# A hybrid encoder step on one core: the second block of the first unit's up weights is loaded early, into two staging tiles

## The chip, the cores and the metric

The kernel runs on 1 core of a Trainium2 chip. The metric is the device time of one execution in microseconds (us); lower is better. The core has TensorE (PE in the profile; PEld is its weight loads), VectorE (DVE), ScalarE (ACT), GpSimd (POOL) and SyncE (SP). SP starts most of the loads and POOL most of the stores. Each engine works through its own list of instructions in order and waits where an instruction needs something that another engine has not yet finished.

## The reference

One inference step of a 2-layer streaming encoder with width 1024, on 1024 prompt frames and 8 x 16 sample frames, 1152 tokens together. Each layer is a mixer (attention, and in layer 0 a convolution too), an output projection with a residual, and then an MLP with a residual:

```python
def rmsnorm(x, g):
    xf = x.astype(jnp.float32)
    r = lax.rsqrt(jnp.mean(xf * xf, axis=-1, keepdims=True) + RMS_EPS)
    return (xf * r).astype(x.dtype) * g

def sq_relu_mlp(h, w_up, w_down):
    return jnp.square(jax.nn.relu(h @ w_up)) @ w_down

        xp = xp + op                       # op: the mixer's output projection
        xp = xp + sq_relu_mlp(rmsnorm(xp, norm_ffn[layer]), w_up[layer], w_down[layer])
```

D_MODEL is 1024 and D_FF is 4096. All data are 32-bit floats. A final RMSNorm and the new caches are outputs too.

## The kernel before, in words

Activations are kept transposed: a tile holds 128 of the 1024 channels by all 1152 tokens. For precision every matrix product is made from pairs. An operand is split into a rounded high part (ACT copies it, line 185) and the rest as a low part (DVE subtracts, line 186), and three matmuls (high by high, high by low, low by high: `SPLIT`) replace one. Weights go through this split as well: a raw block is loaded by SP into a staging tile (tag `st`, a ring of 3 tiles of 128x512) or another raw tile, split into a pair tile (`hl...`), and read by PE.

The change sits at the border between the output projection and the MLP of each layer, in the function `rest`, which runs twice: the first MLP at about 530 us, the second at about 1930 us of the span.

**The output projection's second half.** Its 8 chunks of 128 output channels are numbered n = 0..7; `order` makes them channels 0, 4, 1, 5, 2, 6, 3, 7. The residual of each chunk is loaded into one of four raw tiles `xr0`..`xr3` (`spare`, line 1346). Each chunk has three token groups g of 384. After a group, DVE adds the product to the residual (`evac`, line 1386), ACT squares it (line 1792), and POOL adds the square to a sum (line 1793) that the RMSNorm needs. The chunks 6 and 7 are taken together, group by group. A row of PE that reads `psob` belongs to this projection.

**The MLP's up product** runs in 16 units of 2 blocks of 128 hidden channels. Inputs are cut in 2 x 2: by channel (chunk c and chunk c+4) and by token (two halves of 576), and the two weight blocks of a unit are cut in 2 x 2 too: `a11`, `a12` are the halves of the first block (channels 0..511 and 512..1023), `a21`, `a22` those of the second. Seven products instead of eight are made per unit, by a scheme of the Strassen kind. They need sums of inputs (`combine`, lines 1368 to 1380 and their splits: 11 steps per channel pair c, written into the tiles `b11`, `t2`, `t1`, `b21`, `t3`, `b22`, `t4`) and sums of weights: `s1 = a21 + a22`, then `a21 - a11`, then `s1 - a11` in the place of `a11` (`two_sums`, lines 1412 to 1414), and `a12 - a11` in the place of `a12` (line 1434). `seven(i)` makes the pair tile of product i. Product 0 takes `a11`; 1 takes `s1 - a11`; 2 takes `s1`; 3 takes `a12`; 4 takes `a21 - a11`; 5 takes `a12` after its subtraction; 6 takes `a22`. Products 0, 3 share a PSUM bank of partial sums, 1, 4, 6 another, 2, 5 a third (`um` in the rows, one per token quarter n).

**The first unit.** Its two weight blocks are loaded by `raw(0)` into `xr0` and `xr1` (line 1407), which hold the residual chunks n = 4 and n = 5 until `combine` of the third channel pair has read them. `raw(0)` is started by `evac` behind that combine, and `raw(1)` behind the next one. In the first unit PE makes the products 0, 1, 2 for the channel pairs c = 0..2 first, then the sums of squares for the norm (`ms_m`, line 263), then c = 3 of the products 0, 1, 2, and then the products 3 to 6. After product 0, ACT copies its bank out (line 1507, the rows `tm<-um`); product 3 adds into the same bank, and so starts behind that copy. The norm's factor is made meanwhile: DVE line 268, ACT's square root (line 269, which needs another function table, `ACT_TABLE_LOAD`), a few small DVE steps, a diagonal (line 281) and a product `rr_m` (line 285).

**What sets the order.** The program is written as above, and a scheduler then orders the instructions of each engine from dependences, buffers and its own costs; it keeps the written order only for what is passed to `pinned`. An edit at one place therefore can change the order at others.

Of the kernel before, what the change touches and what calls it, by code (L numbers as in the profile page):

```python
# [17 lines left out]
KC = 8  # L18
# [22 lines left out]
def f(ap):  # L41
    return ap.bitcast(F32)
# [82 lines left out]
def tile_trunk(ctx, tc, ins, outs):  # L125
# [5 lines left out]
    dma = nc.sync.dma_start  # L131
# [51 lines left out]
    def split(hi, lo, src):  # L183

        ACT(hi, src, AF.Copy)  # L185
        return tt(lo, src, f(hi), ALU.subtract)  # L186
# [3 lines left out]
    def staging(src, name, n=512):  # L190
        st = sp.tile([P, 512], F32, tag="st", name=f"st_{name}")
        dma(st[:, :n], src)
        return st
# [161 lines left out]
    class Cat:  # L355
# [5 lines left out]
        def put(self, piece, rows, c0, n):  # L361
            if self.direct is None:
                put(cat_d[self.layer][self.p, rows, c0:c0 + n], piece[rows, :n])
                return
            at = c0
            while at < c0 + n:
                g = at // G
                m = min(c0 + n, g * G + G) - at
                hi, lo = (x[rows, self.p % 4, at - g * G:at - g * G + m] for x in self.direct[g][self.p // 4])
                split(hi, lo, piece[rows, at - c0:at - c0 + m])  # L370
                at += m
# [923 lines left out]
    def rest(layer, ks, cat, rst, mp, then, soon=None):  # L1295
# [7 lines left out]
        name = f"m{layer}"  # L1303

        def own(tag, dtype, n=T):
            return mp.tile([P, n], dtype, tag, f"{tag}{layer}")

        def pair(t, n=1024):

            return t[:, :n].rearrange("p (a t) -> p a t", a=2)  # L1310


        spare = [own(f"xr{n}", F32) for n in range(4)]
# [29 lines left out]
        def old(n):  # L1343
            if n < KC and order[n] not in x:
                x[order[n]] = spare[n % 4]
                dma(x[order[n]], xm_d[layer][:, order[n], :])
# [4 lines left out]
        def some(n):  # L1351
            for go in todo[:n]:
                go()
            del todo[:n]

        def combine(c):

            x1, x2 = x[c], x[c + 4]
            w1, w2 = (norms[:, 2 * layer + 1, k:k + 1] for k in (c, c + 4))
            one, two = slice(0, TW), slice(TW, T)  # L1360
            d, t3, t2, t4 = (t[:, h] for t in temps for h in (one, two))

            def halves(key, src, w):
                hi, lo = (combo(key, c)[:, i] for i in range(2))
                if w is None:
                    split(hi, lo, src)
                else:
                    ACT(hi, src, AF.Copy, scale=w)
                    stt(lo, src, w, f(hi), ALU.mult, ALU.subtract)

            return [lambda: (ACT(t3, x2[:, two], AF.Copy, scale=w2), halves("b11", x1[:, one], w1)),
                    lambda: stt(t3, x1[:, two], w1, t3, ALU.mult, ALU.subtract),
                    lambda: stt(t2, x1[:, one], w1, t3, ALU.mult, ALU.subtract),
                    lambda: halves("t2", t2, None),
                    lambda: tt(d, x1[:, two], x1[:, one], ALU.subtract),
                    lambda: halves("t1", d, w1),
                    lambda: halves("b21", x2[:, one], w2),
                    lambda: halves("t3", t3, None),
                    lambda: halves("b22", x2[:, two], w2),
                    lambda: stt(t4, x2[:, one], w2, t2, ALU.mult, ALU.subtract),  # L1380
                    lambda: halves("t4", t4, None)]

        def evac(n, ps, g):
            fc = order[n]
            xs = x[fc][:, g * G:g * G + G]
            tt(xs, xs, ps[:, :G], ALU.add)
            nx.square(xs, fc, slice(g * G, g * G + G), n == 0, add=nc.gpsimd.tensor_tensor)
            if g == NG - 1:
                put(xr_d[layer][fc], x[fc])
                if n % 2:  # L1390
                    todo.extend(combine(fc - 4))

                    todo.append((lambda: (old(n + 3), old(n + 4))) if n < 4 else (lambda: raw(n // 2 - 2)))
            some(3)
            if n == KC - 1 and g == 1:
                seven(0)


        raws, ups, parts = {}, {}, [0]
        pinned = tc.keep_in_program_order  # L1400

        def raw(m):

            if m < NF // 2 and m not in raws:
                raws[m] = [spare[m % 2 * 2 + e][:, :1024] for e in range(2)]
                for e in range(2):
                    dma(raws[m][e], ins["w_up"][layer, 2 * m + e])

        def two_sums(m, pin=lambda ins: ins):
            a11, a21, a22 = raws[m][0][:, :512], raws[m][1][:, :512], raws[m][1][:, 512:]  # L1410
            s1 = ups["s1"] = sp.tile([P, 512], F32, "st", f"s1{name}{m}")
            pin(tt(s1, a21, a22, ALU.add))
            tt(a21, a21, a11, ALU.subtract)
            tt(a11, s1, a11, ALU.subtract)

        def seven(i):

            if i in ups or i >= 7 * NF // 2:
                return
            m, k = divmod(i, 7)  # L1420
            a1, a2 = raws[m]
            a11, a12, a21, a22 = a1[:, :512], a1[:, 512:], a2[:, :512], a2[:, 512:]
            if k == 0:
                src = a11
            elif k == 1:
                if "s1" not in ups:
                    two_sums(m)
                src = a11
            elif k == 2:
                src = ups.pop("s1")  # L1430
            elif k == 3:
                src = a12
            elif k == 4:
                tt(a12, a12, a11, ALU.subtract)
                src = a21
            else:
                src = a12 if k == 5 else a22
            if i % 6 < 4:
                w = sp.tile([P, 2, 512], F32R, "hl", f"hl_{name}{i}")
            else:  # L1440
                w = pair(few[i % 6 - 4])
            if k == 0 and m:
                pinned(ACT(w[:, 0], src, AF.Copy))
                pinned(tt(w[:, 1], src, f(w[:, 0]), ALU.subtract))
            else:
                split(w[:, 0], w[:, 1], src)
            ups[i] = w
# [12 lines left out]
        def unit(m):  # L1460

            if m:
                raw(m + 1)
# [61 lines left out]
            if m == 0:  # L1525

                for ks in (range(3), range(3, 4)):
                    for k in range(3):
                        for n in range(2):
                            mms(k, n, ks)  # L1530
                            if ks[0]:
                                take(k, n)
                        if not ks[0]:
                            seven(k + 2)
                            some(3)
                    if not ks[0]:
                        some(99)
                        nx.end(0, pin=tc.keep_in_program_order)
                        nx.end(1, pin=tc.keep_in_program_order)
                nx.end(2, pin=tc.keep_in_program_order)  # L1540
                start = 3
            for k in range(start, 7):
                seven(7 * m + k + 2)
                if m and k == 1:
                    last_sum(m - 1)
                if m < NF // 2 - 1 and k == 5:
                    two_sums(m + 1, pinned)
                if m == NF // 2 - 1 and k > 4:
                    begin(k - 5)
                for n in range(2):  # L1550
                    mms(k, n, range(4))
                    if m == 0 and k == 3:
                        nx.rows[n]()
                        if n == 0:
                            continue
                        take(k, 0)
                    if m == 0 and (k, n) == (4, 0):
                        nx.rows[2]()
                    take(k, n)
# [20 lines left out]
        a11, a21, a22, braw, bsplit, asplit, streams, bs, ws, later = ({}, {}, {}, [], [], [], {}, {}, {}, [])  # L1580
# [161 lines left out]
        for n in range(KC - 2):  # L1742
            run(chunk_steps(n, got, ahead, cat, ks, lambda ps, g: evac(n, ps, g), f"ob{layer}{n}", depth=2))
        run(chunks_steps([KC - 2, KC - 1], got, ahead, cat, ks, evac, f"ob{layer}", depth=0))
        seven(1)
        for m in range(NF // 2):
# [239 lines left out]
```

## Time and profile before

| | |
|---|---|
| time before, median of 3 runs | 2727.23 us (2723.51 to 2727.84) |
| time of the profiled execution | 2730.68 us |
| its span | 2728.9 us |
| around the span | 1.8 us |
| mean granted clock of TensorE | 0.993 |

A row of the timeline is: start in us, duration in us, engine, line, operation, output<-inputs, shapes, how many in a row; in brackets the idle time of that engine just ahead of it and what ended it. A row of the waits is: engine, what it was about to do, `<-` what it waited for, total us, number of times, longest. A row of the windows is: stretch, its length, then busy us of each engine with its number of instructions, the granted clock of TensorE (1.00 is full speed), the share of DMA engines that were busy, and GB/s. A matmul's duration reaches past the start of the next one.

### The profile page before, as it was taken

The numbers are of one execution on the slowest core, as the hardware profiler recorded it, in microseconds if no ns is written. First come the engines' busy times: TensorE is split into PE (matmuls) and PEld (weight loads), VectorE is DVE, ScalarE is ACT, GpSimd is POOL, SyncE is SP. The second block draws the span as 40 slices with busy tenths as digits, with TensorE's granted clock in tenths as the row PEclk, the third lists the DMA queues.
The fourth block names the chain that finished last, engine by engine and source line by source line (L and its number), as shares of the span: only waits on it lengthen the run. The fifth ranks groups of instructions, "written<-read, shape, count | busy, mean of one in ns | idle before, by whom it ended". The sixth has DMA issues, their size and how long they took to land.

```text
span 2728.9 us, 50505 instructions
## 1 busy us (share of the span) xinstructions
PE 2662.6 (98%) x19362; PEld 2553.8 (94%) x19362; DVE 2040.6 (75%) x4105; ACT 1365.7 (50%) x2854; POOL 330.5 (12%) x599
## 2 busy tenths in 40 slices
PE   8999998999999999999999999998999999999998
PEld 8888886899999999999999999997999999999998
DVE  7999996787777755768577777778787777647577
ACT  5344456755555543445355555555455555534344
POOL 1000111131111100000011111110321111100001
PEclk9999999999999999999999999999999999999999
DMA  4344447443333486335444444446543334674344
GB/s 159 104 128 149 146 141 241 171 145 141 140 138 138 151 290 224 108 113 178 145 141 139 129 139 141 137 127 218 181 140 138 143 141 147 233 254 135 96 125 146
DMA packets 173203, 422.90 MB, mean 155 GB/s; under 512 B 25968, under 2 KB 53808, under 8 KB 170912
## 3 DMA queue, kind: packets, MB, share of 16 engines
q1 hardware_dynamic: 135696, 288.38, 32.6%
q0 software_dynamic: 37120, 131.27, 13.9%
q8 instruction: 152, 2.49, 0.4%
q14 instruction: 91, 0.75, 0.1%
q10 hardware_dynamic: 144, 0.02, 0.0%
HBM read 289.60 MB, written 117.34 MB: 149 GB/s over the span
## 4 chain that ended last, share of the span: by engine, by line
PE 84%; DVE 7%; ACT 3%; issue 3%; DMA 3%; POOL 0%; SPq 0%; DVEq 0%; ACTq 0%; POOLq 0%
PE pd L1705 26%; PE um L1480 25%; PE psc L225 10%; PE psp L225 4%; PE avc L469 2%; PE tpc L457 2%; PE psoa L225 2%; PE f L225 1%; PE zs L570 1%; PE zc L1220 1%; PE ava L398 1%; DVE y L737 1%; PE so L604 1%; PE psg L225 1%; PE psa L225 1%
## 5 line engine op out<-in xcount | busy, mean ns | idle before, releaser
L225 PE MATMUL psc<-h,hl_wc 128*128 128x384 f32 x1728 | 327.1, 339 | 0.0
L225 PEld LDWEIGHTS psc<-h,hl_wc 128*128 128x128 f32 x1728 | 296.8, 188 | 13.3 <-issue 10.9
L1480 PE MATMUL um<-sl,hl_m 128*128 128x288 f32 x1548 | 240.8, 296 | 0.0
L1480 PEld LDWEIGHTS um<-sl,hl_m 128*128 128x128 f32 x1548 | 218.2, 189 | 0.0
L1705 PE MATMUL pd<-tm,hl_wd 128*128 128x288 f32 x1584 | 214.7, 294 | 0.0
L1705 PEld LDWEIGHTS pd<-tm,hl_wd 128*128 128x128 f32 x1584 | 211.3, 189 | 0.0
L737 DVE SCALAR_TENSOR_TENSOR y<-u,dw,y 128x1024 f32<-128x1024 f32 (+1 forms) x232 | 177.5, 805 | 0.7
L1487 ACT ACTIVATE hdm<-hdm 128x288 f32<-128x288 f32 x192 | 84.7, 442 | 156.4 <-DVE hdm L1486 154.8
L225 PE MATMUL psp<-h,hl_wi 128*128 128x384 f32 x864 | 162.5, 340 | 0.0
L186 DVE TENSOR_TENSOR tm<-xr,tm 128x576 fp32r<-128x576 f32 (+1 forms) x120 | 85.7, 715 | 94.8 <-ACT tm L185 94.6
L225 PEld LDWEIGHTS psp<-h,hl_wi 128*128 128x128 f32 x864 | 148.4, 188 | 6.2 <-issue 5.1
L185 ACT ACTIVATE tm<-xr 128x576 fp32r<-128x576 f32 (+1 forms) x120 | 77.6, 647 | 94.7 <-PE pd L1705 75.9
L1480 PE MATMUL um<-sl,hl 128*128 128x288 f32 x756 | 119.1, 296 | 0.0
L1187 ACT ACTIVATE s<-s,mxc 128x640 f32<-128x640 f32 (+4 forms) x128 | 88.8, 694 | 60.2 <-DVE mxc L1184 58.6
L1705 PE MATMUL pd<-th,hl_wd 128*128 128x288 f32 x792 | 113.9, 297 | 3.8 <-DVE th L186 3.7
L1705 PEld LDWEIGHTS pd<-th,hl_wd 128*128 128x128 f32 x792 | 108.7, 191 | 4.5 <-DVE th L186 4.2
L1705 PE MATMUL pd<-xr,hl_wd 128*128 128x288 f32 x792 | 111.9, 295 | 0.0
L1705 PEld LDWEIGHTS pd<-xr,hl_wd 128*128 128x128 f32 x792 | 107.4, 189 | 0.0
L1480 PEld LDWEIGHTS um<-sl,hl 128*128 128x128 f32 x756 | 106.4, 188 | 0.8
L1705 PE MATMUL pd<-tm,hl 128*128 128x288 f32 x768 | 104.9, 295 | 0.0
L1705 PEld LDWEIGHTS pd<-tm,hl 128*128 128x128 f32 x768 | 103.1, 188 | 0.0
L185 ACT ACTIVATE whc<-tpc 128x512 fp32r<-128x512 f32 (+1 forms) x144 | 72.5, 523 | 46.7 <-PE tpc L457 45.7
(530 smaller groups left out, 6536.8 us busy)
## 6 DMA issues: line engine op xcount, KB each, us to landing
xr<-hb_d SPq DMA_DIRECT2D x208, 288.0 KB, 2.9
xr<-in_w_up_dram SPq DMA_DIRECT2D x64, 512.0 KB, 4.0
hb_d<-hdm POOLq DMA_DIRECT2D x96, 288.0 KB, 2.4
hb_d<-t POOLq DMA_DIRECT2D x96, 288.0 KB, 2.4
wm<-in_w_down_dram SPq DMA_DIRECT2D x64, 256.0 KB, 4.1
st_wd<-in_w_down_dram SPq DMA_DIRECT2D x64, 256.0 KB, 3.5
st_wc<-in_w_in_c_dram SPq DMA_DIRECT2D x44, 256.0 KB, 2.6
xm_d<-xo POOLq DMA_DIRECT2D x16, 576.0 KB, 3.8
```

What stands on the lines that cost most here:

```text
L185: ACT(hi, src, AF.Copy)
L186: return tt(lo, src, f(hi), ALU.subtract)
L225: mm(ps()[:, :G], hl[:, a, at:at + P], act[g][k // 4][b][:, k % 4, :], start=n == 0, stop=n == len(todo) - 1)
L398: mm(st["av"][64 * m:64 * m + 64, o0:o0 + n], vs[:, j, i], st["w"][gi][:, c0:c0 + n], start=gi == 0, stop=gi == last)
L457: nc.tensor.transpose(tp[:, c0 + q * P:c0 + (q + 1) * P], blocks.get(j, tile_q), ident)
L469: mm(st["av"][:, o0:o0 + n], vs[:, j, i].rearrange("p a d -> p (a d)"), src[:, c0:c0 + n], start=st["done"] == 0, stop=st["done"] == nmm - 1)
L570: mm(box["z"][at // 512][own, at % 512:at % 512 + kw], qb[:, own], k[:, b * kw:b * kw + kw], start=True, stop=True)
L737: stt(src if j == CW - 1 else dst, src, wj, dst, ALU.mult, ALU.add)
L1187: ACT(s[:, :n], s[:, :n], AF.Exp, bias=mx, scale=-1.0, accum_out=tot)
L1480: mm(banks[b, n][:, :TQ], w[:, a, c * P:c * P + P], combo(key, c)[:, h, n * TQ:n * TQ + TQ], start=k < 3 and c == 0 and i == 0, stop=c == ...
L1487: ACT(y, y, AF.Relu)
L1705: mm(ps, w[:, a, m * P:m * P + P], b[:, h, (n - ns[0]) * TQ:(n - ns[0]) * TQ + TQ], start=first and s == 0, stop=j == NJ - 1 and s == 2, s ...
```

## The change

Block 1 of the first unit (`a21` and `a22`, 512 KB) is no longer loaded by `raw(0)` into `xr1`. It is loaded in two halves of 256 KB into two tiles of the staging ring, at the first token group of chunk n = 5 (`n == KC - 3`). `raw(0)` loads block 0 alone. All later units load as before. `raws[m]` is now a list of the four quarters. The lines behind the edit move by 13 or 14.

```diff
@@ evac @@
             some(3)
+            if n == KC - 3 and g == 0:
+                raw_second()
             if n == KC - 1 and g == 1:
                 seven(0)
@@ raw @@
             if m < NF // 2 and m not in raws:
-                raws[m] = [spare[m % 2 * 2 + e][:, :1024] for e in range(2)]
+                raws[m] = []
                 for e in range(2):
-                    dma(raws[m][e], ins["w_up"][layer, 2 * m + e])
+                    if m == 0 and e == 1:
+                        raws[m] += second
+                        continue
+                    t = spare[m % 2 * 2 + e][:, :1024]
+                    dma(t, ins["w_up"][layer, 2 * m + e])
+                    raws[m] += [t[:, :512], t[:, 512:]]
+
+        second = []
+
+        def raw_second():
+
+            for half in range(2):
+                second.append(staging(ins["w_up"][layer, 1][:, half * 512:half * 512 + 512], f"{name}r{half}"))
 
         def two_sums(m, pin=lambda ins: ins):
-            a11, a21, a22 = raws[m][0][:, :512], raws[m][1][:, :512], raws[m][1][:, 512:]
+            a11, _, a21, a22 = raws[m]
@@ seven @@
-            a1, a2 = raws[m]
-            a11, a12, a21, a22 = a1[:, :512], a1[:, 512:], a2[:, :512], a2[:, 512:]
+            a11, a12, a21, a22 = raws[m]
```

Below, names carry buffer numbers, which differ between the two programs; lines 1412, 1413, 1414, 1434, 1507 before are 1426, 1427, 1428, 1447, 1520 in the changed kernel. The three places look alike in both MLPs.

On SP, in the changed kernel, between the last staged weights of the output projection and the residual chunks n = 6 and 7:

```order
L192 DMA st_wo0b_1_6058<-in_w_out_ab_dram 128x512
L192 DMA st_m0r_6081<-in_w_up_dram 128x512
L192 DMA st_m0r_6083<-in_w_up_dram 128x512
L1346 DMA xr_5629<-xm_d_112 128x1152
L1346 DMA xr_5630<-xm_d_112 128x1152
L1413 DMA xr_5627<-in_w_up_dram 128x1024
```

The two loads into `st_m0r` are new there, ahead of the two residual loads; of the two loads of `raw(0)` the second is gone.

On DVE before, from the last steps of the last channel pair on (`t3m_50`, `b22m_70`, `t2m_31` are low parts of its input sums, L1434 is `a12 - a11`, `hl_5631` the low part of product 4's weights, L1380 the last input sum, L268 the start of the norm's factor):

```order
L186 TENSOR_TENSOR t3m_50_6335<-tm_5634,t3m_50_6335 128x576
L1369 SCALAR_TENSOR_TENSOR b22m_70_6338<-xr_5630,norms,b22m_70_6338 128x576
L186 TENSOR_TENSOR t2m_31_6302<-tm_5635,t2m_31_6302 128x576
L1434 TENSOR_TENSOR xr_5627<-xr_5627 128x512
L186 TENSOR_TENSOR hl_5631<-xr_5628,hl_5631 128x512
L1380 SCALAR_TENSOR_TENSOR tm_5635<-xr_5630,norms,tm_5635 128x576
L268 TENSOR_SCALAR v_m_6375<-ms_m_6371 128x3
```

and in the changed kernel:

```order
L1447 TENSOR_TENSOR xr_5627<-xr_5627 128x512
L1372 SCALAR_TENSOR_TENSOR tm_5634<-xr_5629,norms,tm_5634 128x576
L1369 SCALAR_TENSOR_TENSOR b22m_70_6341<-xr_5630,norms,b22m_70_6341 128x576
L1373 SCALAR_TENSOR_TENSOR tm_5635<-xr_5629,norms,tm_5634 128x576
L186 TENSOR_TENSOR t3m_50_6338<-tm_5634,t3m_50_6338 128x576
L186 TENSOR_TENSOR hl_5631<-st_m0r_6081,hl_5631 128x512
L186 TENSOR_TENSOR t2m_31_6305<-tm_5635,t2m_31_6305 128x576
L1380 SCALAR_TENSOR_TENSOR tm_5635<-xr_5630,norms,tm_5635 128x576
```

The subtraction of `a12` and the low part of product 4 stood behind `t2m_31` and now stand ahead of it; L1380 follows `t2m_31` directly.

On ACT before, at the same place (`t4m_71` is the high part of the last input sum, `v_m` the square roots, `tm<-um` the copies out of product 0's bank):

```order
L185 ACTIVATE t2m_31_6302<-tm_5635 128x576
L185 ACTIVATE hl_5632<-xr_5627 128x512
L1507 ACTIVATE tm_5634<-um_6279 128x288
L1507 ACTIVATE tm_5634<-um_6289 128x288
L185 ACTIVATE hl_m_6476<-xr_5628 128x512
L185 ACTIVATE t4m_71_6365<-tm_5635 128x576
L269 ACT_TABLE_LOAD
L269 ACTIVATE v_m_6375<-v_m_6375 128x3
L269 ACTIVATE v_m_6389<-v_m_6389 128x3
```

and in the changed kernel:

```order
L185 ACTIVATE t2m_31_6305<-tm_5635 128x576
L185 ACTIVATE t4m_71_6368<-tm_5635 128x576
L269 ACT_TABLE_LOAD
L269 ACTIVATE v_m_6378<-v_m_6378 128x3
L269 ACTIVATE v_m_6392<-v_m_6392 128x3
L1520 ACTIVATE tm_5634<-um_6282 128x288
L1520 ACTIVATE tm_5634<-um_6292 128x288
L269 ACTIVATE v_m_6430<-v_m_6430 128x3
L185 ACTIVATE hl_m_6479<-st_m0r_6083 128x512
```

The two copies out of product 0's bank stood ahead of `t4m_71` and the table load; they now stand behind both and behind two square roots.

## The prediction

> **What bounds the kernel now.** I read the page first, then the waits of TensorE around the edited place in both MLPs, then the timelines there.
>
> ```profile
> span 2728.9 us, 50505 instructions
> PE 2662.6 (98%) x19362; PEld 2553.8 (94%) x19362; DVE 2040.6 (75%) x4105; ACT 1365.7 (50%) x2854; POOL 330.5 (12%) x599
> 700.00:800.00 100.00, 100.00 (x756) 100.00 (x755) 77.40 (x152) 52.59 (x117) 17.28 (x32) 1.00 0.38 137
> ```
>
> PE sets the end; once the MLP's units run (700 to 800 us) it has no gap. So what the first unit gains or loses is carried to the end, and I follow the start of unit 1. PE's waits between the output projection's end and unit 1, first MLP (first two rows), then second MLP (three; two shorter waits stand in PE's rows below):
>
> ```profile
> PE um L1480 <- ACT hl_m L185: 2.5, 1, 2.5
> PE um L1480 <- DVE hl_m L186: 0.4, 1, 0.4
> ...
> PE um L1480 <- ACT hl_m L185: 1.3, 1, 1.3
> PE um L1480 <- DVE t2m L186: 1.0, 1, 1.0
> PE um L1480 <- DVE hl_m L186: 0.7, 1, 0.7
> ```
>
> The waits on `hl_m` (2.9 and 2.0 us) are product 1 waiting for its weights, which need the second block. The others are DVE being late with the last channel pair. DVE's timeline (first MLP two rows, then second) shows why:
>
> ```profile
> 586.13 1.32 DVE L1412 TENSOR_TENSOR s1m<-xr 128x512 f32<-128x512 f32 x1 [1.01 <-DMA xr<-in_w_up_dram]
> 600.44 0.80 DVE L1380 SCALAR_TENSOR_TENSOR tm<-xr,norms,tm 128x576 f32<-128x576 f32 x1
> ...
> 1983.48 1.10 DVE L1380 SCALAR_TENSOR_TENSOR tm<-xr,norms,tm 128x576 f32<-128x576 f32 x1
> 1988.18 1.31 DVE L1412 TENSOR_TENSOR s1m<-xr 128x512 f32<-128x512 f32 x1 [1.02 <-DMA xr<-in_w_up_dram]
> 1993.91 1.05 DVE L186 TENSOR_TENSOR hl_m<-s1m,hl_m 128x512 fp32r<-128x512 f32 x1
> 1995.62 1.50 DVE L186 TENSOR_TENSOR hl_m<-xr,hl_m 128x512 fp32r<-128x512 f32 x1
> 2000.63 0.74 DVE L186 TENSOR_TENSOR t2m<-tm,t2m 128x576 fp32r<-128x576 f32 x1
> 2001.30 0.68 DVE L1434 TENSOR_TENSOR xr<-xr 128x512 f32<-128x512 f32 x1
> 2002.50 0.80 DVE L1380 SCALAR_TENSOR_TENSOR tm<-xr,norms,tm 128x576 f32<-128x576 f32 x1
> ```
>
> DVE waits for the second block once, about 1.0 us, and then has no idle time until the last L1380 ends at 2003.30 (601.24 in the first MLP). It is a second chain beside PE, nearly as long. What PE makes of it:
>
> ```profile
> 590.82 4.21 PE L1480 MATMUL um<-t2m,hl_m 128*128 128x288 f32 x16 [0.35 <-DVE hl_m L186]
> 602.12 1.04 PE L1480 MATMUL um<-sl,hl_m 128*128 128x288 f32 x6
> ...
> 1992.86 2.39 PE L1480 MATMUL um<-t2m,hl_m 128*128 128x288 f32 x16 [0.67 <-DVE hl_m L186]
> 2000.08 0.40 PE L1480 MATMUL um<-t2m,hl_m 128*128 128x288 f32 x1 [0.32 <-ACT t2m L185]
> 2001.42 0.93 PE L1480 MATMUL um<-t2m,hl_m 128*128 128x288 f32 x5 [0.95 <-DVE t2m L186]
> 2003.52 0.80 PE L263 MATMUL ms_m<-ones,accm 128*128 128x1 f32 x6 [0.37 <-DVE v_m L268]
> 2004.18 1.04 PE L1480 MATMUL um<-sl,hl_m 128*128 128x288 f32 x6
> 2019.19 1.08 PE L1480 MATMUL um<-b11m,hl_m 128*128 128x288 f32 x7
> ```
>
> Product 3 starts at 602.12 and 2004.18; from there PE runs to unit 1 (2019.19) in 15.0 us without waits. **So the number to forecast is when product 3 starts.** The same 16 matmuls took 4.21 us in the first MLP and 2.39 in the second: the clock. Here are windows of it, each behind the wait that it follows:
>
> ```profile
> PE f L225 <- ACT h L185: 1.8, 1, 1.8
> 54.00:56.00 2.00, 2.00 (x8) 2.00 (x7) 2.00 (x5) 1.57 (x3) 0.00 (x0) 0.50 0.00 0
> ...
> 591.00:594.00 3.00, 3.00 (x13) 3.00 (x14) 3.00 (x5) 3.00 (x6) 2.96 (x3) 0.50 0.60 243
> ...
> PE psoa L225 <- DVE cpc L479: 2.1, 2, 1.9
> 1901.00:1903.00 2.00, 1.75 (x10) 1.60 (x10) 1.91 (x6) 1.72 (x4) 0.00 (x0) 1.00 0.33 69
> 1997.00:2004.00 7.00, 5.35 (x40) 4.71 (x38) 7.00 (x14) 3.67 (x8) 0.00 (x0) 1.00 0.26 80
> ```
>
> Behind the wait of 1.8 us (at 50 us) and behind the 2.5 us of the first MLP the granted clock is 0.50; behind 1.9 us (at 1900) and behind the short waits of the second MLP it stays 1.00.
>
> **The change part by part (second MLP in full).** *Loads.* Two new loads stand on SP ahead of the residual loads of chunks 6 and 7. Their tiles come free when DVE has split the last staged weights, well before those residual loads can go:
>
> ```profile
> 557.40 0.29 DVE L186 TENSOR_TENSOR hl<-st_wo0b,hl 128x128 fp32r<-128x128 f32 x1
> 563.64 3.64 SPq L1346 DMA_DIRECT2D xr<-xm_d  x2
> 567.16 1.21 DVE L1369 SCALAR_TENSOR_TENSOR b11m<-xr,norms,b11m 128x576 fp32r<-128x576 f32 x1 [0.28 <-ACT b11m L1368]
> 582.50 3.61 DMA xr<-in_w_up_dram
> ```
>
> So nothing is held up, and the bytes are the same: 0 us. If the cover of 6 us were gone, the residuals would be late by an issue or two.
>
> *Removed on DVE.* The wait of 1.02 and `s1` with 1.31 leave the stretch: 2003.30 - 2.33 = 2000.97 for the end of L1380. In the first MLP `s1` lands in a chain of DVE and ACT that has 0.28 us of room (ahead of `b11m` at 567.16) and takes about 0.6, so 0.3 comes back there; in the second it falls into a longer idle time of DVE.
>
> *Added on DVE.* `a21 - a11` now waits for the first block, whose load takes about 3.6 as above, and product 1's low part follows close on ACT's high part: 0.3 us together, 2001.3.
>
> *POOL.* A DVE row that meets a POOL sum of squares is longer: 1.50 and 1.05 us for an operation of the size that takes 0.68 (the row of L1434).
>
> ```profile
> 1987.92 1.02 POOL L1793 TENSOR_TENSOR accm<-accm,t 128x384 f32<-128x384 f32 x1 [0.35 <-ACT t L1792]
> ```
>
> Four such sums fall into this stretch. Before, one lay in DVE's wait, one in `s1` (removed above), and two cost 0.37 and 0.82. Without the wait all four can cost their full 1.02: 0 to 2.04 + 0.65 + 0.20 = 2.9 more. Laid against DVE's new order, a sum is partly covered where DVE drains a bank (L1386); I take 1.8. L1380 then ends at 2003.1 (bounds 2001.3 and 2004.2), against 2003.30: most of what the early load frees is taken again. [...]
>
> *PE's waits.* The waits for `hl_m` go (2.0), so PE is through c = 3 of product 0 at 2000.08 - 0.32 - 1.97 = 1997.8. Next is `t2m`, which now stands behind L1434 and a low part on DVE and directly ahead of L1380: it ends at 2003.1 - 0.8 = 2002.3 (2000.5 to 2003.4) where it was 2001.37. PE idles 4.5 us (2.7 to 5.6) in one piece: longer than any of the waits behind which the clock halved, so I expect 0.50. The work from there to product 3 is 2004.18 - 2001.42 - 0.37 = 2.4 us, at the slow rate (4.21 to 2.39) 4.2. Product 3 at 2006.5: **+2.3 us.**
>
> [...]
>
> *ACT.* Product 3 must also wait for the copies out of product 0's bank, now behind these:
>
> ```profile
> 2002.67 0.71 ACT L1507 ACTIVATE tm<-um 128x288 f32<-128x288 f32 x2
> 2003.79 0.68 ACT L185 ACTIVATE t4m<-tm 128x576 fp32r<-128x576 f32 x1
> 2004.49 1.28 ACT L269 ACT_TABLE_LOAD   x1
> 2005.78 0.30 ACT L269 ACTIVATE v_m<-v_m 128x3 f32<-128x3 f32 x2
> ```
>
> From the end of L1380: 0.68 + 1.28 + 0.30 + half of 0.71 = 2.6, so 2005.7. That is +1.5 even at full clock; at half clock PE comes later than this, and it is covered.
>
> *First MLP* likewise: L1380 ends at 601.24 - 2.33 + 0.3 + 0.3 + 1.8 = 601.3, `t2m` at 600.5, product 3 at 604.7 against 602.12: **+2.6**; by ACT alone 603.9 (+1.8). It already had half clock before, but earlier, where DVE's lateness hid it.
>
> Sum: **+4.9 us.** Lower bound (no new collision, full clock, ACT's order): 2001.3 + 2.6 - 2004.18 = -0.3 and 599.5 + 2.6 - 602.12 = 0.0; upper: 2003.4 + 4.2 - 2004.18 = 3.4 and 3.7. Together -0.3 to +7.1. On the profiled execution 2730.68 becomes 2735.6. That execution was 3.45 above the median shown, so I forecast 2727.23 + 4.9 = 2732.1.
>
> **The rivals.** *Gone in full:* PE was the only bound and keeps what the load frees: 2.9 + 2.0, the later waits of 1.0 + 0.3 + 0.4, and 1.8 (4.21 to 2.39) for the slow clock in the first MLP: -8.4, 2718.8. Against it: DVE is busy 7.00 of 7 us in 1997 to 2004. *ACT's order alone:* the clock stays; +1.5 + 1.8 = 3.3, 2730.5. For it: one 1.9 us wait left the clock alone; against: 4.5 is far longer. *It cancels:* fewer collisions and a shorter idle time, near the lower bound: 2727.0, within 1 us. *More waits:* the norm's steps on DVE are interleaved with sums that read ACT's copies (L1509), and `rr_m` now stands behind 13 matmuls of product 3; if the diagonal comes later than those 1.7 us, PE waits once more, 1 to 2 us per MLP: +8, 2735.5. By the rows it is ready at about the same time, with little to spare.
>
> **How the numbers follow.** Forecast 0.54, own range 2729 to 2734.5; ACT's order alone 0.17; cancels 0.11; gone in full 0.07; more waits 0.11. What this kernel's measurement can tell from no change is about 0.2%, 5.5 us, so 2721.8 to 2732.7 is "same". Of the forecast's 0.54 some 0.28 lies above; with "more waits" slower is 0.39. Faster is 0.07, same 0.54. The range leaves out the gain in full and a part of the worst: 2726 to 2735.5.
>
> **What would show it.** Right: no PE wait on `hl_m` L185 of product 1; a PE wait of 3 to 5.5 us on `t2m` in both MLPs; granted clock 0.5 behind it; product 3 starting some 2 to 3 us later after the projection's last matmul than before; `tm<-um` behind the table load. Wrong: DVE's last L1380 more than 1.5 us earlier relative to the projection's end, PE's wait on `t2m` under 2 us, or clock 1.00 there.

## The result and the profile after

The changed kernel takes 2732.87 us (median of 17 runs, 2727.45 to 2737.82), the kernel before, measured beside it, 2725.47 (17 runs, 2722.92 to 2729.48). The ratio is 1.0023, with a 95% interval of 1.0017 to 1.0029: about 6 us slower (the medians are 7.4 apart), where 4.9 were forecast. The profiled execution took 2736.22, 1.8 more than its span. Both profiled executions took longer than their medians (2736.22 against 2732.87, 2730.68 against 2725.47), so the lengths read from them below belong to these executions.

The head of the page of the changed kernel:

```profile
span 2734.4 us, 50509 instructions
PE 2670.8 (98%) x19362; PEld 2562.0 (94%) x19362; DVE 2044.2 (75%) x4105; ACT 1366.2 (50%) x2854; POOL 330.3 (12%) x599
```

PE has 8 us more busy time for the same 19362 matmuls: some of them ran slower. PE's waits in the first unit, first MLP and then second:

```profile
PE um L1493 <- ACT t2m L185: 3.6, 1, 3.6
PE um L1493 <- DVE t2m L186: 0.6, 1, 0.6
...
PE um L1493 <- ACT t2m L185: 3.6, 1, 3.6
PE um L1493 <- DVE t2m L186: 0.6, 1, 0.6
```

The waits for `hl_m` are gone, and one long wait for `t2m` stands in their place. PE's timeline (start, us; four rows of the first MLP, then the second):

```profile
583.03 2.56 PE L1493 MATMUL um<-b11m,hl_m 128*128 128x288 f32 x18
596.52 0.61 PE L1493 MATMUL um<-t2m,hl_m 128*128 128x288 f32 x1 [3.63 <-ACT t2m L185]
601.69 1.79 PE L1493 MATMUL um<-sl,hl_m 128*128 128x288 f32 x6
618.60 3.34 PE L1493 MATMUL um<-b11m,hl_m 128*128 128x288 f32 x24
...
1989.39 2.56 PE L1493 MATMUL um<-b11m,hl_m 128*128 128x288 f32 x18
2002.44 0.61 PE L1493 MATMUL um<-t2m,hl_m 128*128 128x288 f32 x1 [3.58 <-ACT t2m L185]
2003.66 1.57 PE L1493 MATMUL um<-t2m,hl_m 128*128 128x288 f32 x5 [0.62 <-DVE t2m L186]
2006.47 1.27 PE L263 MATMUL ms_m<-ones,accm 128*128 128x1 f32 x6
2007.61 1.79 PE L1493 MATMUL um<-sl,hl_m 128*128 128x288 f32 x6
2010.87 1.48 PE L285 MATMUL rr_m<-accm,ones 128*128 128x384 f32 x2
2024.67 3.34 PE L1493 MATMUL um<-b11m,hl_m 128*128 128x288 f32 x24
```

And windows around the slow stretch of either MLP (the granted clock, PEclk, is third from the end):

```profile
595.80:606.60 10.80, 9.46 (x36) 8.54 (x37) 7.73 (x28) 4.50 (x10) 0.00 (x0) 0.53 0.47 146
2002.00:2013.00 11.00, 9.94 (x38) 9.02 (x39) 7.53 (x29) 4.58 (x10) 0.00 (x0) 0.53 0.44 143
```

Each window holds the whole stretch at half clock. The clock inside it is 0.50, so it lasted twice the missing share: 2 x 0.47 x 11.0 = 10.3 us, and 10.2 in the first MLP. Product 3 (601.69, 2007.61) lies inside it: its first six matmuls take 1.79 where they took 1.04.

Executions differ ahead of the first unit too (its first matmul came 1.4 us earlier in the first MLP and, behind the first MLP's loss, 1.6 later in the second), so I count from that first matmul (583.03 and 1989.39; 584.41 and 1987.80 before); what happens ahead of it is not in the first three columns. Each pair of numbers below is first MLP / second MLP, from one profiled execution of each kernel; the kernels e1 to e10 are those of the next section. The last two columns are over the timed runs: the median against that of before, and the mean of the mean granted clocks (before: 0.9932 beside e1 to e10).

| kernel | product 3 starts | unit 1 starts | from one to the other | us against before | mean clock |
|---|---|---|---|---|---|
| before | 17.7 / 16.4 | 32.7 / 31.4 | 15.0 / 15.0 | | 0.9932 |
| the change | 18.7 / 18.2 | 35.6 / 35.3 | 16.9 / 17.1 | +7.4 | 0.9908 |
| e1 load alone | 18.0 / 16.1 | 32.7 / 30.8 | 14.7 / 14.8 | -1.1 | 0.9935 |
| e2 copies first | 18.8 / 18.0 | 34.1 / 33.2 | 15.2 / 15.2 | +5.9 | 0.9911 |
| e4 t2 first | 17.4 / 16.1 | 32.8 / 31.4 | 15.4 / 15.4 | +4.1 | 0.9921 |
| e5 copies, fill | 16.9 / 16.2 | 32.9 / 32.1 | 16.0 / 16.0 | +0.7 | 0.9941 |
| e6 no sums | 15.7 / 14.7 | 32.4 / 30.0 | 16.7 / 15.2 | -1.2 | 0.9923 |
| e7 t2 early | 14.3 / 12.9 | 29.4 / 27.9 | 15.1 / 15.0 | -4.1 | 0.9939 |
| e8 t2 early, late load | 15.4 / 14.6 | 30.4 / 31.1 | 15.0 / 16.5 | -1.0 | 0.9936 |
| e9 fill only | 18.0 / 17.6 | 32.8 / 33.9 | 14.8 / 16.3 | +4.7 | 0.9934 |
| e10 t1 early | 12.5 / 11.5 | 28.8 / 27.8 | 16.3 / 16.3 | -8.7 | 0.9950 |

For the change, unit 1 comes 2.85 + 3.89 = 6.7 us later, which is about the whole loss. VectorE and ScalarE around `t2m`, second MLP:

```profile
1989.06 1.39 DVE L1428 TENSOR_TENSOR xr<-s1m,xr 128x512 f32<-128x512 f32 x1
1992.82 1.05 DVE L186 TENSOR_TENSOR hl_m<-xr,hl_m 128x512 fp32r<-128x512 f32 x1
1993.79 1.69 DVE L1375 TENSOR_TENSOR tm<-xr 128x576 f32<-128x576 f32 x1
1998.66 1.55 DVE L1372 SCALAR_TENSOR_TENSOR tm<-xr,norms,tm 128x576 f32<-128x576 f32 x1
2002.26 0.68 DVE L186 TENSOR_TENSOR hl<-st_m1r,hl 128x512 fp32r<-128x512 f32 x1
2002.86 0.75 DVE L186 TENSOR_TENSOR t2m<-tm,t2m 128x576 fp32r<-128x576 f32 x1
2003.53 0.81 DVE L1380 SCALAR_TENSOR_TENSOR tm<-xr,norms,tm 128x576 f32<-128x576 f32 x1
...
597.62 0.81 DVE L1380 SCALAR_TENSOR_TENSOR tm<-xr,norms,tm 128x576 f32<-128x576 f32 x1
...
2005.08 1.28 ACT L269 ACT_TABLE_LOAD   x1
2006.69 0.71 ACT L1520 ACTIVATE tm<-um 128x288 f32<-128x288 f32 x2
```

Four rows take 1.05 to 1.69 where their like takes 0.68 to 0.81; product 4's low part stands ahead of `t2m`'s; the copies stand behind the table load.

### The profile page after: what moved, and what is told of

Read it like the earlier page. It is cut to its first block, busy times and chain, and to the rows that moved or that the text cites. A ratio compares the mean times of both kernels' runs of the same rounds, so it can differ in the third digit from the quotient of the medians.

```text
span 2734.4 us, 50509 instructions
## 1 busy us (share of the span) xinstructions
PE 2670.8 (98%) x19362; PEld 2562.0 (94%) x19362; DVE 2044.2 (75%) x4105; ACT 1366.2 (50%) x2854; POOL 330.3 (12%) x599
## 3 DMA queue, kind: packets, MB, share of 16 engines
q1 hardware_dynamic: 135984, 288.38, 32.7%
## 4 chain that ended last, share of the span: by engine, by line
PE 73%; DVE 3%; ACT 2%; DMA 1%; issue 1%; DVEq 0%; ACTq 0%; SPq 0%
PE pd L1718 26%; PE um L1493 25%; PE psc L225 10%; PE avc L469 2%; PE tpc L457 2%; PE psob L225 2%; PE zc L1220 1%; PE psoa L225 1%; PE zc L1221 1%; PE so L604 1%; PE zs L570 1%; ACT s L1187 0%; DMA cr<-cat_d 0%; DVE xr L1386 0%; DMA xr<-in_w_up_dram 0%
```

## The experiments

My theory: the early load is harmless and the loss has two halves, the long wait for `t2m` (VectorE's new order, lengthened by POOL's sums) and the half clock behind it. Rivals: the two loads disturb something; ScalarE's order alone; POOL's sums alone; VectorE's lateness alone, the clock being harmless.

The scheduler decides the order, so most kernels force one. After the first unit is written down, instructions of one engine are chained by their place in the written order:

```
+        def queue(here, engine, *orders):
+            mine = [i for i in nc.cur_bb.bb.instructions[here:] if i.engine == engine]
+            for order in orders:
+                for a, b in zip(order, order[1:]):
+                    tc.add_manual_dep(mine[b], mine[a].name, mybir.DependencyInfo(
+                        mybir.DependencyClass.NoSync, mybir.DependencyReason.DATA), reason="queue")
```

The chain adds no wait between engines, only an order on one.

**e1: the load alone.** The change, with VectorE's and ScalarE's rows of the projection's end and the first unit chained as the kernel before had them (a table of 95 to 103 places on VectorE and 44 on ScalarE; TensorE's order falls out the same).

> The early load as in the change, but VectorE, ScalarE and TensorE keep the order that they had before. Theory (the new order of the work on VectorE and ScalarE costs the time, the early load itself is harmless): VectorE's wait of 1.02 us for the second block is gone, TensorE's waits on hl_m fall from 2.0 to about 1 us in the second MLP and from 2.9 to about 1.9 in the first, the waits on t2m stay at 0.3 + 1.0, the clock stays at 1.00 in the second MLP; 1 to 2 us per MLP faster than before, together -1 to -4 us, where the change is +6.3. Rival (the two loads in the staging tiles disturb the output projection or hold other loads up): it stays at +4 to +6. Rival (the sums on POOL take all that the wait frees): 0, within 1 us.

Measured: 2725.05 against 2726.12, ratio 0.9994 (0.9985 to 1.0003). So the rival of disturbing loads falls, the time is not at +4 to +6. Whether the load alone gains 1 us or nothing (the second rival) isn't told by this interval. In the trace the waits on `hl_m` fell to 0.67 from 2.0 in the second MLP, below the 1 us expected, but only to 2.5 from 2.9 in the first, where 1.9 was expected; and the clock didn't stay up. PE's timeline in the second MLP:

```profile
1995.76 0.40 PE L1493 MATMUL um<-t2m,hl_m 128*128 128x288 f32 x1 [0.30 <-ACT t2m L185]
1997.11 1.57 PE L1493 MATMUL um<-t2m,hl_m 128*128 128x288 f32 x5 [0.95 <-DVE t2m L186]
```

and the window behind it:

```profile
1996.80:2000.80 4.00, 3.69 (x18) 3.69 (x18) 3.67 (x9) 3.07 (x6) 0.00 (x0) 0.57 0.47 125
```

The same waits of 0.3 and 0.95 had left the clock at 1.00 in the kernel before; here it is halved, for 2 x 0.43 x 4.0 = 3.4 us.

**e2: the copies first.** The change's own order, with the two copies `tm<-um` (places 79 and 80 on ScalarE) moved back ahead of `t4m` (76) and the table load:

```
-    73, 69, 76, 77, 78, 79, 80, 81, ...
+    73, 69, 79, 80, 76, 77, 78, 81, ...
```

> The change, with ScalarE's two copies out of product 0's bank put back ahead of t4m and the table load; everything else on VectorE, ScalarE and TensorE in the change's order. Theory (TensorE at half clock comes to product 3 later than the copies): product 3 starts where it started, 18.2 to 18.7 us behind the unit's first matmul, and the time stays at +5.5 to +6.5 us over the kernel before. Rival (ScalarE's order alone is the loss): product 3 about 1.5 us earlier in each MLP, +3 us over before.

Measured: 2732.03 against 2726.12, ratio 1.0021 (1.0012 to 1.0030). As the theory has it; the rival falls: product 3 starts at 18.8 and 18.0 where the change has 18.7 and 18.2, not 1.5 us earlier, and the time is within the noise of the change's (ratio 1.0023), so ScalarE's order costs nothing here that these intervals can tell. TensorE's order changed too (`rr_m` stands behind 13 matmuls of product 3); here, with the clock back up ahead of product 3 (its first six matmuls take 1.04 in the second MLP), the way from there to unit 1 takes 15.2 us against 15.0 before, so that order is worth some 0.2 us per MLP at most. In its profiled execution the half clock of the second MLP is shorter all the same, 2 x 0.47 x 7.2 = 6.8 us by this window:

```profile
1994.80:2002.00 7.20, 4.29 (x18) 3.98 (x18) 5.86 (x12) 4.35 (x8) 0.00 (x0) 0.53 0.50 152
```

**e3: the wait filled, a miss.** 26 matmuls more, behind c = 3 of product 0:

```
+                        if ks[0] and k == 0:
+                            fill = bank(f"fill{name}")
+                            for _ in range(26):
+                                pinned(mm(fill[:, :TQ], ups[0][:, 0, :P], combo("b11", 0)[:, 0, :TQ], start=True, stop=True))
```

> The change, with 26 matmuls more in each first unit that write a bank nobody reads, between the last channel pair of product 0 and that of product 1, where TensorE waits 3.6 us for t2m; every other order as in the change. Theory (the idle time halves the clock, and half of the loss is work at half clock): granted clock 1.00 through the wait and behind it, product 3 held by ScalarE's copies at some 0.5 us earlier than in the change, and 15.0 us from product 3 to unit 1 in place of 17.0: 2.5 us per MLP, so +1 to +2 us over before. Rival (the clock costs nothing that counts, VectorE's lateness is the whole loss): +6, and 17 us from product 3 to unit 1.

Measured: 2740.52 against 2726.12, ratio 1.0051 (1.0038 to 1.0063). The kernel didn't do what it was for, as its PE timeline shows:

```profile
2005.64 5.24 PE L1549 MATMUL fillm<-b11m,hl_m 128*128 128x288 f32 x26 [5.64 <-DVE v_m L268]
```

The new bank comes free only when VectorE has read the norm's sums (L268), which stands behind L1380; so the fill waited 5.64 us, and the granted clock was 0.50 for the first 3.4 us of it, up to 2009.1. It tells nothing between the theories. e5 repeats it without that wait.

**e4: t2 first.** The change, with the last pair's `t3`, `t2` sums and `t2m` directly behind the last drained bank on VectorE, the rest behind them, and the copies early on ScalarE (72, 73 the last drained banks, 83 L1375, 74 `b11`, 84 `t1`, 75 L1372, 76 L1373, 82 `t2m`, 87 `t3m`, 86 `b21`; on ScalarE 65 L1371, 64 the last square, 69 `t2m`, 73 `t3m`, 79 and 80 the copies):

```
+    VectorE: 72, 83, 74, 73, 84, 75, 76, 82, 87, 86, then 88 to 91, 93, 101
+    ScalarE: 71, 66, 63, 70, 65, 64, 72, 69, 73, 79, 80, 74, 75, 76, 77, 78
```

> The change, with the steps for t2 of the last channel pair put first on VectorE and ScalarE (L1372, L1373 and the low part of t2m directly behind the last drained bank; b22, t3, a12 and product 4's split behind them) and the copies out of product 0's bank ahead of the table load. Theory: t2m is ready some 2.5 us earlier, TensorE waits for it 2 us or less, the clock stays at 1.00, product 3 starts 13.5 to 14.5 us behind the unit's first matmul (16.4 and 17.7 before, 18.2 and 18.7 in the change), and the norm's steps may take 1 us per MLP of it back: -4 to -7 us against before. Rival (something other than VectorE's order holds t2m, the evictions or the sums on POOL): product 3 no earlier than 16.4 us, 0 to +3 us over before.

Measured: 2730.17 against 2726.12, ratio 1.0015 (1.0005 to 1.0024): below the change by the medians, though the intervals overlap, and on the wrong side of my numbers. The first step did work: `t2m`'s low part was ready 11.7 us behind the first matmul in place of 14.2 (second MLP), and PE's wait shrank (its timeline, second MLP):

```profile
1994.76 0.55 PE L1493 MATMUL um<-t2m,hl_m 128*128 128x288 f32 x1 [1.54 <-ACT t2m L185]
1995.55 1.57 PE L1493 MATMUL um<-t2m,hl_m 128*128 128x288 f32 x5 [0.24 <-DVE t2m L186]
```

The window there:

```profile
1994.80:1998.40 3.60, 3.36 (x12) 2.84 (x12) 3.57 (x6) 1.26 (x3) 0.00 (x0) 0.53 0.51 146
```

Behind this wait of 1.54 us the clock was halved again (for 2 x 0.47 x 3.6 = 3.4 us), and a new wait of 0.68 stands ahead of `ms_m` (VectorE's L268 had moved back). The profiled execution (2726.11) is the fastest of this kernel's eleven, so the mean clock of all of them, 0.9921 between the change's 0.9908 and 0.9932 before, says more: over all of them, the shorter wait still goes with less clock than before.

**e5: copies first, and the wait filled.** e2 with 33 extra matmuls into the columns that a bank of product 2 leaves unused:

```
+                            for _ in range(33):
+                                mm(banks[2, 0][:, TQ:], ups[0][:, 0, :P], combo("b11", 0)[:, 0, :512 - TQ], start=True,
+                                   stop=True, skip_group_check=True)
```

With them three of the twelve outputs are other numbers, here and in e9 (by 0.23 to 0.25, relative); the work that is timed is otherwise that of e2.

> The copies-first kernel with 33 matmuls more per first unit, between product 0's and product 1's last channel pair, that write the unused columns of a bank of product 2 (in the filled kernel the extra matmuls wrote a bank of their own, and waited 4.6 and 5.6 us for that bank; here nothing is waited for). Same order otherwise. Theory (half of what the long wait costs is the half clock behind it): granted clock 1.00 there, no longer wait, product 3 some 16.5 us behind the unit's first matmul in place of 18.0 and 18.8, 1.5 to 2 us per MLP less than the copies-first kernel, which is +5.7: so +2 to +3 us over before, and a mean granted clock of 0.993 to 0.994 in place of 0.991. Rival (the clock takes nothing, since work at half clock hides behind VectorE): +5.5 or more.

Measured: 2727.38 against 2726.71, ratio 1.0006 (0.9996 to 1.0015). Only the fill differs from e2 (1.0021): 4 us come back by the ratios and 5 by the medians, by more work on PE. Its PE timeline and a window in the second MLP:

```profile
1993.49 3.84 PE L1548 MATMUL um<-b11m,hl_m 128*128 128x224 f32 x33
2003.31 0.88 PE L285 MATMUL rr_m<-accm,ones 128*128 128x384 f32 x2 [1.02 <-DVE v_m L273]
```

```profile
1993.00:2003.00 10.00, 8.58 (x69) 8.13 (x68) 9.23 (x24) 5.84 (x12) 1.10 (x1) 1.00 0.58 195
```

The clock is 1.00 throughout; so the half clock was a loss of its own, and the rival that calls it harmless falls. PE at full clock now meets the next late thing, 1.0 us ahead of `rr_m`.

**e6: no sums.** The change's order, with POOL's sums left out for the last two chunks:

```
-            nx.square(xs, fc, slice(g * G, g * G + G), n == 0, add=nc.gpsimd.tensor_tensor)
+            nx.square(xs, fc, slice(g * G, g * G + G), n == 0,
+                      add=nc.gpsimd.tensor_tensor if n < KC - 2 else lambda *a: None)
```

> The change in its own order on VectorE, ScalarE and TensorE, without POOL's sums of squares for the last two chunks (left out of the computation, so the norm is another number). Theory (POOL's sums lengthen VectorE's rows): the rows that took 1.39, 1.05, 1.69 and 1.55 us take 0.7 to 0.8, VectorE's last L1380 ends some 2.5 us earlier, TensorE waits some 1.5 to 2 us for t2m in place of 4.2, product 3 starts 2 to 3 us earlier per MLP: -1 to +2 us against before. Rival (the sums cost VectorE nothing that TensorE notices): +5 to +6 as the change.

Measured: 2725.54 against 2726.71, ratio 0.9990 (0.9981 to 1.0000), at the lower edge of what the theory has. The rows that took 1.69 and 1.55, and what is left of PE's wait, in the timeline of the second MLP:

```profile
1986.51 0.75 DVE L1375 TENSOR_TENSOR tm<-xr 128x576 f32<-128x576 f32 x1
1990.43 0.81 DVE L1372 SCALAR_TENSOR_TENSOR tm<-xr,norms,tm 128x576 f32<-128x576 f32 x1
1993.47 0.40 PE L1494 MATMUL um<-t2m,hl_m 128*128 128x288 f32 x1 [0.36 <-ACT t2m L185]
1994.69 1.57 PE L1494 MATMUL um<-t2m,hl_m 128*128 128x288 f32 x5 [0.82 <-DVE t2m L186]
```

PE's wait for `t2m` falls from 4.2 to 1.2 us (2.1 in the first MLP), product 3 starts 2.9 and 3.5 us earlier. The kernel lacks 12 sums in all, so this is at most the price of the collisions.

**e7: t2 early.** The early load with an order made for it: both last banks drained first, then `b11` and `t2`, and only then `d`, `t3`, `t1`; the norm's first steps (93, 101) ahead of `t1` (85 is product 3's low part; 88 and 89 only have to follow 86):

```
+    VectorE: 80, 81, 72, 73, 74, 75, 76, 85, 82, 83, 87, 93, 101, 84, 86, 90, 91
+    ScalarE: 68, 66, 65, 71, 63, 69, 73, 64, 70, 72, 79, 80, 74, 75, 76, 77, 78
```

**e8: the same order, late load.** The same two chains on the kernel before.

> The early load with an order of its own on VectorE and ScalarE: both last banks are drained first, then b11 and t2 of the last channel pair, then d, t3 and t1 of it; the squares of the last banks go behind t2m on ScalarE, the copies out of product 0's bank ahead of the table load, and the norm's first steps ahead of t1. Theory: t2m's low part is ready 7 us behind the unit's first matmul (12.0 in the t2-first kernel), before TensorE comes to it at 9; no wait over 0.5 us, granted clock 1.00, unit 1 starts 28 to 29.5 us behind the first matmul (32.7 and 31.4 before): -4 to -8 us against before. Rival (the delayed squares hold ms_m and the norm's rows, or POOL's sums fall on t2's steps): 1 to 2 us per MLP come back, -1 to -3.

> The kernel before, with the second block's load where it was, and the same new order of the last channel pair on VectorE and ScalarE as in the t2-early kernel. It tells what the early load itself is worth once the order is right. Theory (the wait for the second block holds TensorE on hl_m for 2.0 and 2.9 us and halves the clock in the first MLP): -1 to -3 us against before, 3 to 5 us more than the t2-early kernel. Rival (the early load is worth nothing, the order everything): the two agree within 1.5 us.

Measured: e7 2722.66, e8 2725.67, before 2726.71; ratios 0.9977 (0.9968 to 0.9986) and 0.9991 (0.9983 to 1.0000). In the right order the early load is worth 3 us, at the lower end of what I expected; the intervals overlap a little. e7's timeline of PE, second MLP, and a window over its whole first unit:

```profile
1990.80 0.96 PE L1493 MATMUL um<-t2m,hl_m 128*128 128x288 f32 x6
1993.02 0.94 PE L1493 MATMUL um<-t1m,hl_m 128*128 128x288 f32 x5 [0.46 <-DVE t1m L1369]
```

```profile
1981.50:2009.40 27.90, 27.03 (x193) 25.47 (x193) 26.96 (x65) 18.90 (x40) 6.19 (x8) 1.00 0.35 121
```

`t2m` isn't waited for (it is ready at 8.3, not at the 7 that I had hoped for, and PE comes at 9.3); two short waits on `t1m` are left, and the clock stays up. In e8's timeline (second MLP, then first) the wait on `hl_m` is back:

```profile
1987.51 0.53 PE L1480 MATMUL um<-t2m,hl_m 128*128 128x288 f32 x2 [0.70 <-ACT hl_m L185]
...
585.21 0.53 PE L1480 MATMUL um<-t2m,hl_m 128*128 128x288 f32 x2 [1.44 <-ACT hl_m L185]
585.94 3.87 PE L1480 MATMUL um<-t2m,hl_m 128*128 128x288 f32 x16 [0.20 <-DVE hl_m L186]
```

The last row, 3.87 us for 16 matmuls that take 2.4 at full clock, shows what follows that wait in the first MLP: a granted clock of 0.53 in 586.20 to 589.80.

**e9: the fill only.** e5 with ScalarE's order as in the change.

> The change with the 33 extra matmuls of the copies-and-fill kernel, and ScalarE's order as in the change (the copies out of product 0's bank behind the table load). Theory (ScalarE's order is a loss of its own that half clock covered): TensorE at full clock now comes to product 3 before the copies, waits there, and starts it some 17.6 us behind the unit's first matmul in place of 16.2 and 16.9; 1 to 1.5 us per MLP more than the copies-and-fill kernel, which came out at +0.7 to +1.6 us, so +3 to +5 us over before. Rival (ScalarE's order costs nothing at any clock): +0.5 to +2.

Measured: 2731.21 against 2726.51, ratio 1.0017 (1.0008 to 1.0027): 4.0 us more than e5 by the medians, as the theory has it, though the two intervals overlap. ScalarE's copies and PE behind them, in its timeline of the second MLP, and PE at the same place in the first:

```profile
2002.71 0.71 ACT L1520 ACTIVATE tm<-um 128x288 f32<-128x288 f32 x2
2003.17 1.69 PE L1493 MATMUL um<-sl,hl_m 128*128 128x288 f32 x6 [1.21 <-ACT tm L1520]
...
597.43 1.07 PE L1493 MATMUL um<-sl,hl_m 128*128 128x288 f32 x6 [1.20 <-ACT tm L1520]
```

So where PE comes at full clock it waits 1.2 us for ScalarE's copies in each MLP. What that costs differs: in the second MLP the clock halves behind the wait (1.69 for the six matmuls, granted clock 0.61 in 2002.80 to 2007.20) and unit 1 starts 1.8 us later than in e5; in the first the clock stays up (1.07 for the six, granted clock 1.00 from 575 to 615), e5's wait of 1.0 us ahead of `rr_m` is gone in exchange, and unit 1 starts no later (32.8 against 32.9). The two together are 1.7 us in the traces, 4.0 by the medians; the size is open. In e2 the loss was invisible, because PE came later than the copies anyway.

**e10: t1 early.** e7 with `t1`'s steps pulled ahead of product 3's weights:

```
-    VectorE: ..., 75, 76, 85, 82, 83, 87, 93, 101, 84, 86, 90, 91
+    VectorE: ..., 75, 76, 83, 82, 84, 85, 93, 101, 87, 86, 90, 91
-    ScalarE: 68, 66, 65, 71, 63, 69, 73, 64, 70, ...
+    ScalarE: 68, 66, 65, 63, 71, 69, 70, 73, 64, ...
```

> The t2-early kernel with the two steps for t1 of the last channel pair ahead of product 3's weights on VectorE and directly behind t2m's high part on ScalarE. In the t2-early kernel TensorE still waited 0.76 + 0.45 and 0.41 + 0.46 us for t1m. Theory: these waits go, product 3 starts 12.1 to 13.4 us behind the first matmul (14.3 and 12.9 there), -7 to -9 us against before (-4 to -6 for t2-early by its medians). Rival (product 3's own weights or the norm come late instead, or the sums on POOL move onto the new order): the same as t2-early within 1.5 us, with a new wait ahead of product 3.

Measured: 2717.86 against 2726.51, ratio 0.9966 (0.9953 to 0.9978). This beats both kernels. PE's timeline of the second MLP, and a window over its first unit:

```profile
1984.53 0.96 PE L1493 MATMUL um<-t2m,hl_m 128*128 128x288 f32 x6
1985.33 0.96 PE L1493 MATMUL um<-t1m,hl_m 128*128 128x288 f32 x6
1994.52 2.38 PE L285 MATMUL rr_m<-accm,ones 128*128 128x384 f32 x6 [1.08 <-DVE accm L281]
```

```profile
1975.20:2003.00 27.80, 26.72 (x195) 25.41 (x194) 26.83 (x65) 19.18 (x40) 5.95 (x8) 1.00 0.35 122
```

PE waits for neither `t2m` nor `t1m`, the clock stays up, and product 3 starts at 12.5 and 11.5. One new wait of 1.08 us, for the norm, stands between product 3 and unit 1.

## Why the prediction was right, and where its sum was off

*Loads, 0 us.* Right: with the old order around it (e1) the load costs nothing that can be measured.

*VectorE.* The last L1380 was to end 0.2 us earlier in the second MLP and 0.1 later in the first, counted from the first matmul. It ended 14.95 us (second MLP) and 15.40 us (first) behind that matmul, 0.55 and 1.43 earlier (2003.30 - 1987.80 = 15.50 and 601.24 - 584.41 = 16.83 before). So the mechanism held (what the wait frees, the sums take) and the second MLP was right within 0.4; the first was 1.5 too pessimistic, just short of the 1.5 us earlier that I had named as a sign of being wrong.

*POOL's sums.* The four rows above are 0.70 + 0.37 + 0.93 + 0.74 = 2.7 us over their like, against 0.37 + 0.82 before: 1.6 more, where 1.8 was taken. The drains (L1386), which I took to cover a part of a sum, take 0.54 to 0.56 us in all 48 rows of before, also beside a sum (the row at 1983.02, beside the one from 1982.50 to 1983.97). e6 shows what the sums are worth to PE: at most 3.0 us of the wait in the second MLP and 2.1 in the first.

*PE's waits.* Right: none on `hl_m`, and 3.58 + 0.62 = 4.2 us on `t2m` (3.63 + 0.61 in the first MLP) where 4.5 was forecast.

*Half clock.* Right that it comes, and e5 against e2 shows it matters. The size is the step that failed: I let it end ahead of product 3 (2.4 us of work becoming 4.2) and kept "from there PE runs to unit 1 in 15.0 us". It lasted 10.2 us in the profiled execution and ran through product 3 and `rr_m`: 16.9 and 17.1, so 4.0 us were missing from the sum. In turn product 3 came later by 0.95 and 1.84 where I had 2.6 and 2.3 (and 2 to 3 as a sign of being right, which neither MLP showed), 2.1 too much, most of it the first MLP's VectorE above. 4.9 + 4.0 - 2.1 = 6.8, against 6.7 measured. That two errors of opposite sign half cancel is luck, and so is the rest of the closeness of 2732.1 to 2732.87: the median of before came out 1.8 under the one that I had started from.

The ground that I gave for the clock, the length of one wait (4.5 us against the 1.8 and 2.5 behind which it had halved), led to the right answer here but is no measure: in e1 it was halved at waits of 0.3 and 0.95, which had left it at 1.00 before, and in e9 it was halved behind 1.21 us in the second MLP and stayed at 1.00 behind 1.20 in the first. It isn't the length of one wait that decides alone.

*ScalarE's order, 1.5 and 1.8 us, covered by half clock.* Right that it is covered: nothing that can be told in e2. Uncovered, in e9 against e5, product 3 starts 1.1 us later in the first MLP and 1.5 in the second, against the 1.8 and 1.5 that I had put on it; what of that reaches the end is open, as said there.

*The rivals.* "ACT's order alone" falls with e2, "it cancels" with the interval, "more waits" with the trace (no wait ahead of `rr_m` in the change; one of 1.0 to 1.1 us appears in e5 and e10, where PE comes earlier). "Gone in full" needed VectorE to be no second chain. With VectorE's steps in an order that makes it none, e10, the time is 8.7 us under that of before (6 to 13 by the interval); the price I had put on it was 8.4. That the two are so near is no proof of its parts: in the profiled executions unit 1 comes 7.6 us earlier, with a new wait for the norm in it.

## What to carry to other kernels

When a load is moved ahead, look in the new order for what the engine behind it does with the time: here a scheduler spent it on work that nobody waited for and put the one sum that PE waits for last. Price a wait of the matrix engine at its length and, where the trace shows half clock behind it, the work there too (in e1 and e4 the half clock lasted 3.4 us; full of work, that is 1.7 us lost by my estimate), and judge the two together with what they cover (ScalarE's late copies cost nothing until the clock was up). Moving a load and ordering its consumers are one change: apart they gave -1 (e1) and -1 us (e8), neither clear of nothing, together -4 (e7).

## What was not expected of the hardware

The half clock was not equally long in the kernels. By the windows shown it lasted 3.4 us in e1 and e4, 6.8 in e2, and 10.2 to 10.3 in the change. What sets these lengths was not shown by any run.

The same kernel also fares differently from run to run: the 27 runs of the kernel before beside e1 to e4 spread from 2719.78 to 2731.61, with a mean granted clock of 0.995 in the fastest and 0.992 in the slowest. As an estimate, with all that is missing of the clock taken as half clock, 0.001 of the mean clock is 2 x 0.001 x 2725 = 5.5 us at half clock, up to 2.7 us lost. The change's 0.9932 - 0.9908 = 0.0024 is up to 6.5 us.

What brings the clock back is not settled. In the change this window is full of work at a clock of 0.50, and the clock was 0.50 up to 2012.40 all the same, with PE busy throughout:

```profile
2005.70:2009.00 3.30, 3.30 (x17) 3.30 (x16) 1.54 (x10) 2.39 (x7) 0.00 (x0) 0.50 0.83 290
2009.00:2012.40 3.40, 3.40 (x13) 2.79 (x13) 2.21 (x12) 0.01 (x1) 0.00 (x0) 0.50 0.01 4
```

So 6.7 us of work without a gap stood at half clock there; what ended it was not shown.
